# Up and down products of a conv feed-forward layer on one core: the first Strassen pair taken by hand-ordered seven products, quarter sums from one load of the rows, down rows and weights split ahead

## The chip, the cores and the metric

The kernel runs on one core of one Trainium2 chip. The metric is the device time of one execution in microseconds (us), the median of several runs. The profile is one execution, taken by the hardware profiler.

## The reference

One layer of a streaming encoder on 1056 tokens (1024 of a prompt and 32 of a decode group, which share the weights). It mixes tokens by a gated linear attention and a banded softmax attention, then runs a convolutional feed-forward network, then a gated embedding. Everything is float32. The change lies in the feed-forward part:

```python
h = rms_norm(x, g_pre_ffn)                      # D_MODEL = 1024
a, g = split(h @ w_up, [D_FF])                  # D_FF = 2816
gx = concat([conv_s0, g], axis=1)
gc = conv_b + sum(conv_w[i] * gx[:, i:i + T] for i in range(3))
y = (gelu(gc) * a) @ w_down
x = x + rms_norm(y, g_post_ffn)
```

Outputs are the layer's rows, the newest attention keys and values, and the two new states.

## The kernel before

**Number format.** Float32 products are made of two reduced operands per value: `hi` is a rounded copy (ScalarE), `lo` is the value less `hi` (VectorE or GpSimd), and a block product is three matmuls: hi times hi, hi times lo, lo times hi. Every tile that TensorE reads has to be split so first, the weights as well as the rows.

**Layout.** Rows are kept transposed: 128 features by 1056 tokens, 8 such tiles for 1024 features (KT = 8, HK = 4 is half of them). `hh` and `hl` hold the split rows of the normed input. The 5632 columns of w_up are 22 pairs f (FT = 22): 128 columns of g (called gx) and the 128 of a (called av).

**Two kinds of up product.** A plain pair is 2 x 3 = 6 products (j picks g or a, three token chunks of 352), each 8 x 3 = 24 matmuls of 352 columns: `up_plain` (L1212) makes pairs 0 to 2 in 18 products, chunks 0 and 1 first, `up_one` (L1201) makes pair 3 (UP_PLAIN = 4). `plain_out` (L1191) copies each product out of PSUM on ScalarE. From pair 4 on, `up_strassen` (L1286) splits rows and weights in quarters and makes a pair by seven products instead of eight (Strassen's scheme in Winograd's form), each 4 x 3 x 2 = 24 matmuls of 264 columns. Its row operands are b11, b21, b22 (quarters of `hh`, `hl`) and the sums t1 = b12 - b11, t2 = b22 - t1, t3 = b22 - b12, t4 = b21 - t2. Its weight operands are quarters and four sums (L1295), each split on ScalarE (L1302) and VectorE (L1303). Results go out of PSUM pairs `two` by sums on VectorE and copies on ScalarE (L1374, L1386).

**Where the sums come from.** The normed rows are also spilled to DRAM (`d_hn`, by the norm, L1095). `quarter_sums` (L1250) loads two tiles for each k of 4 from there (L1242) and makes t1 and t2 (L1256, L1257); `quarter_third` loads them again for t3 (L1267); `quarter_last` loads them a third time for t4 (L1278 to L1280), and writes t4's split over the place of b12 in `hh`/`hl`. Tiles for the loads are two buffers `hn`.

**Activation.** `activate` (L1159) makes the convolution (ScalarE L1164, VectorE L1165 and L1166), the Gelu (ScalarE L1169) and the product with a (VectorE L1170, L1171), then writes the result rows to DRAM (`d_b`, GpSimd's queue). `row_sums` (L1176) later makes quarter sums of them for the down product.

**Order.** Each engine runs its instructions in the order of its queue. The order of TensorE, VectorE and ScalarE is the order of the code wherever `tc.manual_schedule` is entered; it ends behind `up_plain`, and a scheduler sets the order of `up_one` to the last but one `up_strassen`. The last pair and the down product are in code order again. `norm_part` gives the steps of the norm of the last chunk to the first nine plain products; `plain_rest` is stepped behind products 11 to 17 and makes t1, t2 and the activation of pair 0. SyncE's queue carries loads, GpSimd's the loads and stores of `d_b`.

**Down product.** It too is made by seven products. Its row operands are entries e: two row tiles of 528 columns, loaded by GpSimd's queue from `d_b` (`load_entry`, L1434 when written for an up stage tile or `uraw`) and split (`split_entry`, L1446 ScalarE, L1447 VectorE). Weights come per unit u (`load_weights`, `split_weights`, L1456 and L1457), even units into `whi`/`wlo`, odd ones into `dhi`/`dlo`. `ahead(m)` lets the last up pair split the first four entries and unit 0's weights between its products; `last_up[2]` is the rest of that pair's sums (L1367, L1368, L1332 to L1334). `down_unit(u)` makes a unit's matmuls (L1527). `places` names the four PSUM pairs in the order in which the units' chains use them.

Of the kernel before, what the change touches and what calls it, by code (L numbers as in the profile page):

```python
# [98 lines left out]
UP_PLAIN = 4  # L99
# [10 lines left out]
def emit(tc, a):  # L110
# [920 lines left out]
    def norm_steps(tmp, c, z, acc, g, resid, keep, g_next, dst, spill=None):  # L1031
# [60 lines left out]
        for i in range(KT // 2):  # L1092
            times(i, g_next, rstd(s))
            if spill is not None:
                po.dma_start(both(spill, i), zs[i])  # L1095
            ac.activation(dst(i)[0], zs[i], AF.Copy)
            if i:
                low_half(i - 1)
            yield
# [60 lines left out]
    def activate(f, gx, av):  # L1160
        gc = tl(fp, [P, GW - 2], tag="gc", bufs=1)
# [6 lines left out]
        po.tensor_copy(convo[:, f, 2:4], gx[:, GW - 2 : GW])  # L1168
        ac.activation(gc, gc, AF.Gelu_apprx_tanh)  # L1169
# [31 lines left out]
    def up_one(f):  # L1201
        gx, av = up_buffers(f)
        for j in range(2):
            hi, lo = weights(a["w_up"][f + FT * (1 - j)], ve)
            for c in range(NC):
                s = chunk(c)
                ps = ps_mm()[:, : s.stop - s.start]
                product(ps, hi, lo, [(k, k) for k in range(KT)], lambda k: hh[:, k, s], lambda k: hl[:, k, s])
                plain_out(gx, av, j, s, ps)
        return gx, av  # L1210

    def up_plain():  # L1212
# [3 lines left out]
        for i, (f, j, c) in enumerate(steps):  # L1216
# [7 lines left out]
            if i < 9:  # L1224
                norm_part(UP_STEPS[i])
            elif i >= 11:
                next(rest, None)
            if i % 2 == 0 and 1 + i // 4 < 3:
                up_weights(1 + i // 4, i // 2 % 2)
            if i == 8:  # L1230
                rest = plain_rest(bufs)
            plain_out(gx, av, j, s, ps)
# [6 lines left out]
    def quarter_rows(k):  # L1239
        b = [tl(sp, [P, T], tag="hn", bufs=2) for i in range(2)]  # L1240
        for i in range(2):
            dma.dma_start(b[i], d_hn[k + HK * i])  # L1242
        return b[0][:, one], b[0][:, two], b[1][:, one], b[1][:, two]

    def quarter_split(n, k, t):
        h, l = (v[:, k] for v in XS[n])
        ac.activation(h, t, AF.Copy)
        ve.tensor_tensor(l, t, h, op=ALU.subtract)

    def quarter_sums():  # L1250
        for n in ("t1", "t2"):
            XS[n] = [tl(sp, [P, HK, HT], F32R, tag=n + x) for x in "hl"]
        for k in range(HK):
            b11, b12, b21, b22 = quarter_rows(k)
            t1, t2 = [tl(sp, [P, HT], tag="xs", bufs=2) for i in range(2)]
            ve.tensor_tensor(t1, b12, b11, op=ALU.subtract)  # L1256
            ve.tensor_tensor(t2, b22, t1, op=ALU.subtract)  # L1257
            quarter_split("t1", k, t1)
            quarter_split("t2", k, t2)
            yield  # L1260

    def quarter_third():
        XS["t3"] = [tl(sw, [P, HK, HT], F32R, tag="t3" + x) for x in "hl"]
        for k in range(HK):
            b11, b12, b21, b22 = quarter_rows(k)
            t = tl(sp, [P, HT], tag="xs", bufs=2)
            ve.tensor_tensor(t, b22, b12, op=ALU.subtract)  # L1267
            quarter_split("t3", k, t)

    def quarter_last():  # L1270
        XS["b11"] = [t[:, up1, one] for t in (hh, hl)]
        XS["b21"] = [t[:, up2, one] for t in (hh, hl)]
        XS["b22"] = [t[:, up2, two] for t in (hh, hl)]
        XS["t4"] = [t[:, up1, two] for t in (hh, hl)]
        for k in range(HK):
            b11, b12, b21, b22 = quarter_rows(k)
            t = tl(sp, [P, HT], tag="xs", bufs=2)
            ve.tensor_tensor(t, b12, b11, op=ALU.subtract)  # L1278
            ve.tensor_tensor(t, b22, t, op=ALU.subtract)
            ve.tensor_tensor(t, b21, t, op=ALU.subtract)  # L1280
            quarter_split("t4", k, t)

    ROW_JOBS = {min(2 * i + 3 + (i < 2) * (2 - i), FT - 2): row_sums(i, hn_tile) for i in range(FH - 1)}

    def up_strassen(f, ahead=None):
        raw = [raw_weight(), raw_weight() if f == UP_PLAIN else tl(sw, [P, KT, P], tag="sraw", bufs=2)]  # L1286
# [115 lines left out]

    def plain_rest(bufs):
        nonlocal sp
        zp.release()
        sp = pool("sp", side="right")
        yield from quarter_sums()
        activate(0, *bufs[0, 0])
        yield
# [3 lines left out]
    order.__exit__(None, None, None)  # L1413
    uw.release()
    sw = pool("sw")
    for f in range(3, UP_PLAIN):
        open_[f, 0] = up_one(f)
    quarter_third()
    for f in range(1, 3):
        activate(f, *open_[f, 0])  # L1420
    quarter_last()
    for f in range(3, UP_PLAIN):
        activate(f, *open_[f, 0])
    repsum((0, 0, 4))
    for f in range(UP_PLAIN, FT - 1):
# [60 lines left out]
    for e in range(2):  # L1486
        load_entry(e, hn_tile)
    last_up = up_strassen(FT - 1, ahead)
# [35 lines left out]
    places = [chain(j) for j in (3, 2, 0, 1)]  # L1524
# [192 lines left out]
    for e in range(4, 7):  # L1717
# [4 lines left out]
    load_entry(7)  # L1722
# [5 lines left out]
    split_weights(1)  # L1728
    activate(FT - 1, *last_up[:2])
# [6 lines left out]
    for u in range(len(UNITS)):  # L1736
        if u:
            down_unit(u, MID.get(u))
        if u + 2 < len(UNITS):
            load_weights(u + 2)  # L1740
        if 0 < u < len(UNITS) - 1:
# [338 lines left out]
```

## Time and profile before

| | |
|---|---|
| median of 3 runs | 1980.6 us (1978.6 to 1981.62) |
| profiled execution | 1979.3 us |
| its span in the profile | 1977.6 us |
| granted TensorE clock, mean | 0.991 of full speed |
| TensorE busy | 1925.8 us, 97% of the span |
| VectorE, ScalarE, GpSimd busy | 64%, 48%, 23% |
| plain up products | from about 1155 to 1253 us of the span |
| up products by seven | to 1631 us |
| down product | from 1631 us |

Times within the trace count from the start of the span. A group row gives line, engine, operation, tiles and shapes, then busy us and mean ns of one instruction, then the idle time before them and what ended it. A row of waits gives engine, tile and line, then what it waited for: us in total, times, the longest. The mean of a matmul is its latency; matmuls are pipelined, so their rate is read from their number in a full window.

### The profile page before, as it was taken

To read this page: it belongs to the slowest core of one execution; us is meant where nothing else is said; L and a number is where in the kernel's file an instruction comes from. 1 tells how busy PE (TensorE), PEld (TensorE's weight loads), DVE (VectorE), ACT (ScalarE), POOL (GpSimd) and SP (SyncE) were. 2 spreads that over 40 slices of the span, in tenths; PEclk is the share of its full clock that TensorE was granted. 3 is DMA by queue.
4 is the path that set the end of the run, shared out by engine and by line. 5 is a ranking of instruction groups with operands and counts; after the bars stand their busy time and mean duration, and the time that the engine had idled before them with its cause. 6 is when DMAs were issued, how large, how long until landed. Compare 5 with 4: busy or idle time off the path is not lost.

```text
span 1977.6 us, 34638 instructions
## 1 busy us (share of the span) xinstructions
PE 1925.8 (97%) x13584; PEld 1888.0 (95%) x13584; DVE 1260.6 (64%) x2500; ACT 943.2 (48%) x1706; POOL 462.5 (23%) x556
## 2 busy tenths in 40 slices
PE   9999999999999999999999999999999999999996
PEld 8999999999999999999999999999999999999996
DVE  6556556456366475466655677787777776456777
ACT  6356455455364463564434455333333445445444
POOL 2423333232112121211120111232122222115211
PEclk9999999999999999999999999999999999999998
DMA  7323345353444221226787247654334348556679
GB/s 265 100 86 121 100 132 143 99 147 104 113 146 115 81 66 60 97 87 236 255 291 241 89 160 232 218 180 137 130 128 138 123 162 306 183 185 200 202 233 222
DMA packets 107582, 312.04 MB, mean 158 GB/s; under 512 B 13268, under 2 KB 35612, under 8 KB 107292
## 3 DMA queue, kind: packets, MB, share of 16 engines
q1 hardware_dynamic: 81612, 222.99, 34.1%
q0 software_dynamic: 24976, 85.96, 14.6%
q8 instruction: 106, 1.74, 0.4%
q10 hardware_dynamic: 832, 0.90, 0.1%
q14 instruction: 56, 0.46, 0.1%
HBM read 226.34 MB, written 106.52 MB: 168 GB/s over the span
## 4 chain that ended last, share of the span: by engine, by line
PE 69%; DVE 11%; issue 10%; DMA 4%; ACT 4%; POOL 1%; SPq 0%; POOLq 0%; ACTq 0%; DVEq 0%
PE mm L230 10%; PE mm L229 10%; PE mm L231 10%; PE c L1527 7%; PE two L1312 6%; PE two L1313 6%; PE two L1314 6%; DMA hn<-d_hn 3%; PE aux L1527 2%; PE two L835 2%; PE one L601 2%; DVE z L1633 1%; PE one L559 1%; PE two L543 1%; PE one L849 1%
## 5 line engine op out<-in xcount | busy, mean ns | idle before, releaser
L231 PE MATMUL mm<-xh,wlo 128*128 128x352 f32 x1248 | 413.7, 331 | 0.0
L229 PE MATMUL mm<-xh,whi 128*128 128x352 f32 x1248 | 412.9, 331 | 0.0
L230 PE MATMUL mm<-xl,whi 128*128 128x352 f32 x1248 | 410.5, 329 | 0.0
L209 POOL TENSOR_TENSOR wlo<-raw,whi 128x512 fp32r<-128x512 f32 x128 | 181.0, 1418 | 686.8 <-ACT whi L208 630.5
L229 PEld LDWEIGHTS mm<-xh,whi 128*128 128x128 f32 x1248 | 236.1, 189 | 1.9 <-DVE ev L460 0.8
L230 PEld LDWEIGHTS mm<-xl,whi 128*128 128x128 f32 x1248 | 235.7, 189 | 1.7 <-issue 0.3
L231 PEld LDWEIGHTS mm<-xh,wlo 128*128 128x128 f32 x1248 | 235.5, 189 | 1.3
L1312 PE MATMUL two<-mh,whi 128*128 128x264 f32 x576 | 163.1, 287 | 5.8 <-ACT av L1193 2.4
L1314 PE MATMUL two<-mh,wlo 128*128 128x264 f32 x576 | 164.5, 287 | 0.0
L1313 PE MATMUL two<-ml,whi 128*128 128x264 f32 x576 | 164.2, 286 | 0.0
L208 ACT ACTIVATE whi<-raw 128x512 fp32r<-128x512 f32 x140 | 87.0, 628 | 149.7 <-PE mm L230 90.9
L1527 PE MATMUL c<-mh,wlo 128*128 128x264 f32 x438 | 124.5, 284 | 0.8 <-DMA wlo<-d_g 0.8
L1527 PE MATMUL c<-ml,whi 128*128 128x264 f32 x438 | 124.1, 283 | 0.9 <-DVE ml L1447 0.9
L1527 PE MATMUL c<-mh,whi 128*128 128x264 f32 x438 | 124.5, 284 | 0.0
L1312 PEld LDWEIGHTS two<-mh,whi 128*128 128x128 f32 x576 | 108.6, 190 | 6.7 <-ACT av L1193 2.7
L1314 PEld LDWEIGHTS two<-mh,wlo 128*128 128x128 f32 x576 | 109.8, 191 | 0.0
L1313 PEld LDWEIGHTS two<-ml,whi 128*128 128x128 f32 x576 | 109.7, 190 | 0.0
L460 DVE TENSOR_TENSOR ev<-mm,rstd 128x352 f32<-128x352 f32 x120 | 61.3, 519 | 50.4 <-PE mm L231 46.7
L1527 PEld LDWEIGHTS c<-mh,wlo 128*128 128x128 f32 x438 | 82.2, 188 | 1.5 <-DMA wlo<-d_g 1.5
L1527 PEld LDWEIGHTS c<-ml,whi 128*128 128x128 f32 x438 | 82.5, 188 | 1.1 <-DVE ml L1447 1.1
L1302 ACT ACTIVATE whi<-ws 128x512 fp32r<-128x512 f32 x72 | 45.3, 628 | 80.2 <-PE two L1313 48.1
L1527 PEld LDWEIGHTS c<-mh,whi 128*128 128x128 f32 x438 | 82.5, 188 | 0.0
(516 smaller groups left out, 5459.4 us busy)
## 6 DMA issues: line engine op xcount, KB each, us to landing
raw<-in_w_in SPq DMA_DIRECT2D x52, 512.0 KB, 3.7
uraw<-d_b POOLq DMA_DIRECT2D x34, 528.0 KB, 5.0
raw<-in_w_up SPq DMA_DIRECT2D x27, 512.0 KB, 3.6
hn<-d_hn SPq DMA_DIRECT2D x24, 528.0 KB, 4.9
d_b<-av POOLq DMA_DIRECT2D x44, 264.0 KB, 2.7
d_s<-in_w_down POOLq DMA_DIRECT2D x16, 704.0 KB, 7.9
draw<-d_s SPq DMA_DIRECT2D x16, 704.0 KB, 4.1
hn<-d_b POOLq DMA_DIRECT2D x40, 264.0 KB, 3.9
```

Source lines behind the costliest of these rows:

```text
L208: ac.activation(hi[-1][:, d], raw[:, b], AF.Copy)
L209: eng.tensor_tensor(lo[-1][:, d], raw[:, b], hi[-1][:, d], op=ALU.subtract)
L229: pe.matmul(ps, h, xh(kt), start=(first and i == 0), stop=False)
L230: pe.matmul(ps, h, xl(kt), start=False, stop=False)
L231: pe.matmul(ps, l, xh(kt), start=False, stop=(last and i == n - 1))
L460: return lambda ps, s: ve.tensor_tensor(t[:, s], ps, rstd(s), op=ALU.mult)
L601: pe.matmul(ps[:, j0 * P : j1 * P], vs[:, k, vd], got[x][:, k - kb, j0:j1], start=(i == 0 and x == "h"), stop=(i == len(work) - 1 and x == ...
L1302: ac.activation(h, x, AF.Copy)
L1312: pe.matmul(ps[:, j, :HC], w[0][:, k], x[0][:, k, s], start=st, stop=False, skip_group_check=True)
L1313: pe.matmul(ps[:, j, :HC], w[0][:, k], x[1][:, k, s], start=False, stop=False, skip_group_check=True)
L1314: pe.matmul(ps[:, j, :HC], w[1][:, k], x[0][:, k, s], start=False, stop=sp_, skip_group_check=True)
L1527: pe.matmul(ps, w, x, start=st, stop=sp_, skip_group_check=True)
```

## The change

- UP_PLAIN is 3: `up_one` is gone, and pair 3 is made by `up_first`, seven products in the code's own order, with weights and activations of pairs 0 and 1 written between them. `order.__exit__` moves behind it. Its products run X by b11, V by b21, Y by t2, Z by t1, V by t3, X by b22, V by t4.
- The rows are loaded once per k (`quarter_load`, L1239 of the changed file) into tiles `hx`, `gc` and two `hn`, and summed in place: t1, t2, t4. t1 and t2 are split at once. t4 goes raw to DRAM (`d_t4`), and is read back by two loads (L1265) and split once b12's place in `hh` is free. t3 is made by GpSimd (`third_sum`, L1268) from four loads of half rows (L1265).
- The activation is a generator of two steps (convolution; Gelu and product). `plain_rest` is stepped from product 8 on and behind `plain_out`. The last chunk's norm takes its tiles in the order 0, 2, 1, 3.
- Down transition: entry 2 goes into the tile `hx`, entries 3 and 4 into `hn`, each loaded one step earlier; unit 1's weights are split and unit 2's loaded ahead of the last up pair's remaining sums; unit 2's are split between the two steps of the last activation; `places` is (1, 0, 2, 3) instead of (3, 2, 0, 1).

ScalarE before, about the end of the plain products and the start of the first seven products (Gelu L1169, plain evictions L1193 to L1199 into av and gx, split of a t sum L1247, weight split L1302, convolution L1164, product eviction L1374):

```order
L1169 ACTIVATE gc_13103<-gc_13103 128x1058
L1193 ACTIVATE av_12878<-mm_12980 128x352
L1247 ACTIVATE t3h_13058<-xs_13088 128x528
L1164 ACTIVATE gc_13154<-gx_12877,vec_70 128x1058
L1193 ACTIVATE av_12878<-mm_13006 128x352
L1302 ACTIVATE whi_13244<-ws_13209 128x512
L1169 ACTIVATE gc_13154<-gc_13154 128x1058
L1302 ACTIVATE whi_13273<-raw_13169 128x512
L1193 ACTIVATE av_12878<-mm_13032 128x352
L1247 ACTIVATE mh_10372<-xs_13118 128x528
L1302 ACTIVATE whi_13304<-ws_13302 128x512
L1374 ACTIVATE p_2133_13177<-two_13179 128x528
```

And after, in the same place (L1176 is the Gelu, L1170 the convolution, L1201 to L1207 plain evictions, L1294 weight splits and L1331 the first eviction of `up_first`; t3h and mh are the splits of t3 and t4):

```order
L1176 ACTIVATE gc_12791<-gc_12791 128x1058
L1201 ACTIVATE av_12529<-mm_12867 128x352
L1294 ACTIVATE whi_12941<-ws_12939 128x512
L1170 ACTIVATE gc_12946<-gx_12372,vec_70 128x1058
L1247 ACTIVATE t3h_12901<-hn_12754 128x1056
L1331 ACTIVATE p_2089_12907<-two_12909 128x528
L1294 ACTIVATE whi_12978<-ws_12937 128x512
L1247 ACTIVATE t3h_12901<-hn_12823 128x1056
L1294 ACTIVATE whi_13014<-ws_13012 128x512
L1294 ACTIVATE whi_13048<-ws_13046 128x512
L1294 ACTIVATE whi_13104<-raw_12586 128x512
L1247 ACTIVATE mh_10372<-hn_12984 128x2x528
```

The last plain eviction no longer stands behind a Gelu that comes after the last plain products; a split of t3 stands ahead of the weights w3, w4 and w22; both halves of t4 are split in one place.

SyncE's queue before, from the third round of row loads (hn) on to the weights of the seven products (raw):

```order
L1242 DMA hn_13114<-d_hn_11241 128x1056
L1242 DMA hn_13115<-d_hn_11241 128x1056
L1242 DMA hn_13124<-d_hn_11241 128x1056
L1242 DMA hn_13125<-d_hn_11241 128x1056
L1242 DMA hn_13134<-d_hn_11241 128x1056
L1288 DMA raw_13406<-in_w_up 128x1024
L1242 DMA hn_13135<-d_hn_11241 128x1056
L1242 DMA hn_13144<-d_hn_11241 128x1056
L1288 DMA raw_13657<-in_w_up 128x1024
L1242 DMA hn_13145<-d_hn_11241 128x1056
L1288 DMA raw_13908<-in_w_up 128x1024
```

And after, from the last whole rows through half rows and t4 (d_t) to the weights of pair 4 (raw, sraw):

```order
L1239 DMA hn_12715<-d_hn_11241 128x1056
L1265 DMA hx_12752<-d_hn_11241 128x2x528
L1265 DMA hn_12754<-d_hn_11241 128x2x528
L1265 DMA hn_12823<-d_hn_11241 128x2x528
L1361 DMA sraw_13167<-in_w_up 128x1024
L1265 DMA hx_12833<-d_hn_11241 128x2x528
L1361 DMA sraw_13404<-in_w_up 128x1024
L1265 DMA hn_12984<-d_t_1997_12191 128x2x528
L1265 DMA hn_13019<-d_t_1997_12191 128x2x528
L1361 DMA raw_13166<-in_w_up 128x1024
L1361 DMA raw_13403<-in_w_up 128x1024
```

The row loads are fewer; t4's loads stand ahead of raw of pair 4.

VectorE before, at the down transition (ml is a split of an entry, L1367 to L1334 the last up pair's sums, dlo unit 1's weights):

```order
L1447 TENSOR_TENSOR ml_10373<-hn_17499,mh_10372 128x1056
L1447 TENSOR_TENSOR ml_10373<-uraw_17618,mh_10372 128x1056
L1447 TENSOR_TENSOR ml_10373<-uraw_17620,mh_10372 128x1056
L1367 TENSOR_TENSOR c_2632_17353<-p_2631_17352,two_17369 128x528
L1368 TENSOR_TENSOR gx_17348<-gx_17348,c_2632_17353 128x528
L1332 TENSOR_TENSOR gx_17348<-c_2632_17353,two_17370 128x264
L1333 TENSOR_TENSOR gx_17348<-c_2632_17353,two_17370 128x232
L1334 TENSOR_TENSOR gx_17348<-c_2632_17353,two_17370 128x32
L1457 TENSOR_TENSOR dlo_17707<-draw_17611,dhi_17706 128x512
L1457 TENSOR_TENSOR dlo_17711<-draw_17611,dhi_17710 128x512
L1457 TENSOR_TENSOR dlo_17715<-draw_17611,dhi_17714 128x384
```

And after (L1565 entries, L1575 weights, L1440 to L1405 the sums):

```order
L1565 TENSOR_TENSOR ml_10373<-hn_17465,mh_10372 128x1056
L1565 TENSOR_TENSOR ml_10373<-hn_17498,mh_10372 128x1056
L1575 TENSOR_TENSOR dlo_17628<-draw_17610,dhi_17627 128x512
L1575 TENSOR_TENSOR dlo_17632<-draw_17610,dhi_17631 128x512
L1575 TENSOR_TENSOR dlo_17636<-draw_17610,dhi_17635 128x384
L1565 TENSOR_TENSOR ml_10373<-uraw_17617,mh_10372 128x1056
L1440 TENSOR_TENSOR c_2618_17352<-p_2617_17351,two_17368 128x528
L1441 TENSOR_TENSOR gx_17347<-gx_17347,c_2618_17352 128x528
L1405 TENSOR_TENSOR gx_17347<-c_2618_17352,two_17369 128x264
L1406 TENSOR_TENSOR gx_17347<-c_2618_17352,two_17369 128x232
L1407 TENSOR_TENSOR gx_17347<-c_2618_17352,two_17369 128x32
```

Unit 1's weights moved ahead of entry 5 and of the last pair's sums, and entries 3 and 4 come from `hn`.

```diff
-UP_PLAIN = 4
+UP_PLAIN = 3
...
-        for i in range(KT // 2):
+        left = []
+        for i in range(KT // 2) if c < NC - 1 else (0, 2, 1, 3):
...
+        yield
         ac.activation(gc, gc, AF.Gelu_apprx_tanh)
...
-            elif i >= 11:
-                next(rest, None)
...
             if i == 8:
                 rest = plain_rest(bufs)
-            plain_out(gx, av, j, s, ps)
+            if i >= 8:
+                next(rest)
...
+    def quarter_load(k):
+        b = (hn_tile(), hn_tile()) if k % 2 else (odd_tile(), tl(fp, [P, GW - 2], tag="gc", bufs=1)[:, :T].rearrange("p (k t) -> p k t", k=2))
+        for i in range(2):
+            dma.dma_start(b[i], d_hn[k + HK * i].rearrange("p (k t) -> p k t", k=2))
+        XS["rows", k] = b
+    def quarter_first(k):
+        x, y = XS["rows", k]
+        ve.tensor_tensor(x[:, 0], x[:, 1], x[:, 0], op=ALU.subtract)
+        one_ = quarter_split("t1", k, x[:, 0])
+        ve.tensor_tensor(y[:, 1], y[:, 1], x[:, 0], op=ALU.subtract)
+        two_ = quarter_split("t2", k, y[:, 1])
+        ve.tensor_tensor(y[:, 0], y[:, 0], y[:, 1], op=ALU.subtract)
+        po.dma_start(d_t4[k], y[:, 0])
+        one_()
+        two_()
+    def halves(src, k, n, h=slice(0, HT)):
+        t = XS[n] = odd_tile() if n[0] == "b12" else hn_tile()
+        dma.dma_start(t, src[k : k + 2, :, h].rearrange("k p t -> p k t"))
+    def third_sum(j):
+        po.tensor_tensor(XS["b22", j], XS["b22", j], XS["b12", j], op=ALU.subtract)
...
+        for k in range(HK):
+            quarter_first(k)
+            if k < 2:
+                quarter_load(k + 2)
+            elif k == 2:
+                halves(d_hn, 0, ("b12", 0), two)
+                halves(d_hn, HK, ("b22", 0), two)
+            if k == HK - 1:
+                act = activation_steps(0, *bufs[0, 0])
+                next(act)
+            yield
+        halves(d_hn, HK + 2, ("b22", 1), two)
+        next(first)
+        third_sum(0)
+        halves(d_hn, 2, ("b12", 1), two)
+        yield
+        next(act)
...
+    next(first)
+    next(act)
+    lo = third_split(0)
+    next(first)
+    third_sum(1)
+    lo()
+    halves(d_t4, 0, ("t4", 0))
+    lo = third_split(1)
+    next(first)
+    lo()
+    halves(d_t4, 2, ("t4", 1))
+    next(first)
+    next(first)
+    next(first)
+    fourth(0)
+    fourth(1)
+    next(first)
+    next(act)
+    order.__exit__(None, None, None)
...
         if m < 5:
             split_entry(m - 3)
-            load_entry(m - 1, hn_tile)
+            load_entry(m, hn_tile)
...
+    load_entry(2, odd_tile)
...
-    places = [chain(j) for j in (3, 2, 0, 1)]
+    places = [chain(j) for j in (1, 0, 2, 3)]
...
-    for e in range(4, 7):
+    for e in range(5, 8):
         load_entry(e)
...
     split_entry(4)
-    load_entry(7)
+    split_weights(1)
+    load_weights(2)
     split_entry(5)
     load_entry(8)
     last_up[2]()
     slots.append((more[:, :, 0], more[:, :, 1]))
     down_unit(0)
-    split_weights(1)
-    activate(FT - 1, *last_up[:2])
+    act = activation_steps(FT - 1, *last_up[:2])
+    next(act)
+    split_weights(2)
+    for i in act:
+        pass
```

More of the change, by code (lines that the diff above doesn't have):

```diff
@@ L1262, in quarter_third @@
[L1262 to L1281, printed above, removed]
@@ L1400, in emit @@
     sp = None
+    first = up_first()
     def plain_rest(bufs):
@@ L1412, in emit @@
     open_ = up_plain()
-    order.__exit__(None, None, None)
+    repsum((0, 0, 4))
     uw.release()
     sw = pool("sw")
[L1416 to L1419, printed above, removed]
-        activate(f, *open_[f, 0])
[L1421 to L1425, printed above, removed]
+    XS["t3"] = [tl(sw, [P, HK, HT], F32R, tag="t3" + x) for x in "hl"]
+    act = activation_steps(1, *open_[1, 0])
+    next(first)
[14 more added lines that the diff above has]
+    fourth(1)
+    next(first)
+    next(act)
+    order.__exit__(None, None, None)
+    for f in range(2, UP_PLAIN):
+        activate(f, *open_[f, 0])
+    activate(UP_PLAIN, *XS["first"])
+    for f in range(UP_PLAIN + 1, FT - 1):
         up_strassen(f)
```

138 lines of the change are left out of this document (105 added, 33 removed).

## The prediction

> **What bounds the kernel now.** I read the page first, then the stretch of the up product by windows, then what TensorE waited for there, then the clock.
>
> ```profile
> span 1977.6 us, 34638 instructions
> PE 1925.8 (97%) x13584; PEld 1888.0 (95%) x13584; DVE 1260.6 (64%) x2500; ACT 943.2 (48%) x1706; POOL 462.5 (23%) x556
> PE 69%; DVE 11%; issue 10%; DMA 4%; ACT 4%; POOL 1%; SPq 0%; POOLq 0%; ACTq 0%; DVEq 0%
> ```
>
> TensorE is busy 97% of the span and makes 69% of the chain that ended last. An edit helps by fewer matmuls, by a gap closed, or by a clock kept up. The windows of the stretch that the change rewrites (columns: length, busy time and number of instructions of each engine, granted clock, DMA share, GB/s):
>
> ```profile
> 1190.00:1230.00 40.00, 40.00 (x249) 40.00 (x248) 28.44 (x43) 19.90 (x36) 6.42 (x14) 1.00 0.70 231
> 1256.00:1268.00 12.00, 12.00 (x88) 12.00 (x88) 8.15 (x14) 2.94 (x5) 1.08 (x2) 0.86 0.63 213
> 1280.00:1301.00 21.00, 18.75 (x139) 18.54 (x140) 18.27 (x31) 7.21 (x12) 12.23 (x19) 0.92 0.61 202
> 1301.00:1321.50 20.50, 20.50 (x171) 20.50 (x169) 15.21 (x25) 7.66 (x12) 4.78 (x12) 1.00 0.51 172
> 1321.50:1342.00 20.50, 20.50 (x171) 20.50 (x170) 15.78 (x25) 7.51 (x12) 5.15 (x12) 1.00 0.53 164
> ```
>
> The first row is plain product, full: 40.00 / 249 = 0.161 us a matmul of 352 columns. The last two are seven products, full: 41.00 / 342 = 0.120 us a matmul of 264. Between them TensorE loses time; what it waited for from 1225 to 1300:
>
> ```profile
> PE two L1312 <- ACT av L1193: 2.4, 1, 2.4
> PE two L1312 <- ACT p L1374: 2.0, 1, 2.0
> PE two L1312 <- ACT mh L1247: 1.2, 1, 1.2
> PE two L1312 <- DVE gx L1334: 0.2, 1, 0.2
> ```
>
> That is 5.8 us idle in four gaps. The second cost is the clock; slices of 3.41 us around the two large gaps and the third:
>
> ```profile
> 1253.62:1257.03 3.41, 1.56 (x12) 1.56 (x13) 2.30 (x5) 2.33 (x4) 2.29 (x2) 1.00 0.66 213
> 1257.03:1260.44 3.41, 3.41 (x18) 3.41 (x17) 3.41 (x6) 0.72 (x2) 0.72 (x2) 0.50 0.73 240
> 1260.44:1263.85 3.41, 3.41 (x30) 3.41 (x30) 1.52 (x3) 1.04 (x2) 0.35 (x1) 1.00 0.83 307
> 1277.51:1280.92 3.41, 2.24 (x18) 2.03 (x17) 2.84 (x5) 0.73 (x2) 0.89 (x2) 1.00 0.17 68
> 1287.75:1291.16 3.41, 1.39 (x12) 1.18 (x11) 3.30 (x6) 2.58 (x4) 1.61 (x3) 1.00 0.94 275
> 1291.16:1294.58 3.42, 3.42 (x17) 3.42 (x17) 3.42 (x6) 1.12 (x2) 1.49 (x4) 0.50 0.58 210
> ```
>
> Where TensorE was busy 1.56 and 1.39 of 3.41 us, the next slice ran at 0.50 and started 18 and 17 matmuls instead of 30; where it was busy 2.24, the clock stayed. The two halved slices cost (12 + 13) x 0.120 = 3.0 us. So 5.8 + 3.0 = 8.8 us are lost here beside the work itself.
>
> **Why the gaps stand there.** ScalarE around the first gap (start, length, line, tiles, idle time before), then around the second:
>
> ```profile
> 1253.46 1.09 ACT L1169 ACTIVATE gc<-gc 128x1058 f32<-128x1058 f32 x1 [1.83 <-DVE gc L1166]
> 1254.45 0.61 ACT L1302 ACTIVATE whi<-raw 128x512 fp32r<-128x512 f32 x1
> 1254.97 0.44 ACT L1193 ACTIVATE av<-mm 128x352 f32<-128x352 f32 x1
> 1255.32 0.64 ACT L1247 ACTIVATE mh<-xs 128x528 fp32r<-128x528 f32 x1
> ...
> 1288.58 1.27 ACT L1164 ACTIVATE gc<-gx,vec 128x1058 f32<-128x1058 f32 x1 [3.89 <-DVE gx L1394]
> 1289.76 0.59 ACT L1374 ACTIVATE p<-two 128x528 f32<-128x528 f32 x1
> ```
>
> The last plain eviction (L1193) stands behind a Gelu (L1169) that idled 1.83 us for VectorE; the seven-product block after it needs that PSUM. In the second gap the eviction L1374 stands behind a convolution start (L1164) that idled 3.89 us. The third gap (1.2) is the split of t4 (L1247), which waits for rows loaded for the third time:
>
> ```profile
> L1242 SPq DMA_DIRECT2D hn<-d_hn x24: 319/320/673, 1197.8 to 1272.9; - x24
> DMA to landing us min/median/max: 3.9/4.9/7.0
> ```
>
> **The change, part by part.** All times are of the profiled execution, 1979.3 us (span 1977.6), which is 1.3 below the median of the runs, 1980.6.
>
> *Fewer matmuls.* Pair f=3 was 6 products of 24 matmuls: 144 x 0.161 = 23.2 us. Now it is 7 x 24 = 168 x 0.120 = 20.2 us. **-3.0.** This is certain as far as TensorE stays fed.
>
> *The four gaps and two halved slices.* The first gap goes: the new block's first product waits only for the eviction of the 17th of 18 plain products, and no plain block follows. The t4 rows are no longer computed behind three loads each. The second gap came of work of VectorE that had gathered (18.27 busy of 21.00, quoted above); the activations of pairs 0 and 1 now stand inside the plain products and the new block. **-8.8** if nothing takes their place.
>
> *VectorE.* Removed: 4 x 10 sums and splits of 528 columns. Added: 4 x 5 of them, 4 splits of 1056, 7 more weight sums and splits, and 6 PSUM sums for f=3. Rows for these:
>
> ```profile
> L1256 DVE TENSOR_TENSOR xs<-hn 128x528 f32<-128x528 f32 x4 | 2.8, 705 | 2.6 <-DMA hn<-d_hn 2.6
> L1303 DVE TENSOR_TENSOR wlo<-ws,whi 128x512 fp32r<-128x512 f32 x24 | 16.5, 686 | 0.0
> 1636.89 2.62 DVE L1447 TENSOR_TENSOR ml<-uraw,mh 128x1056 fp32r<-128x1056 f32 x2 [3.45 <-ACT mh L1446]
> ```
>
> That is 40 x 0.70 = 28 out, and 20 x 0.70 + 4 x 1.31 + 13 x 0.70 = 28 in: no relief in sum, only another place. So I cost it at nothing by itself; its cover is the 11 us of each 40 that VectorE is idle in the first window above.
>
> *Loads.* 24 loads of 528 KB become 8, 4 of half rows and 2 of t4, with 4 writes of t4 (264 KB). Traffic falls, in windows with a DMA share of 0.6 to 0.7: nothing, or a small gain that I don't count. The order of the last norm chunk (0,2,1,3) and the step at i >= 8 change no count; their cover is the same idle quarter of VectorE.
>
> *New waits in the fixed order.* E is the end of the plain products. The chain to t3: the step with the first third_sum stands behind the 16th of 18 products; GpSimd starts it when its two half-row loads have landed, which I put at E-4 (their tiles come free about E-9, and 4.9 to land). Then third_sum 2.5, the load of b12 of the other half into the tile that it frees 4.9, third_sum 2.5, then on ScalarE the t3 split 1.1 and, behind it in the queue, the split of the weight w3 0.6, then VectorE's part 0.7. Prices:
>
> ```profile
> L652 POOL TENSOR_TENSOR ev<-ev,ev x4: 2462/2480/2696, 183.2 to 424.4; 128x1056 f32<-128x1056 f32 x4
> L209 POOL TENSOR_TENSOR wlo<-raw,whi x128: 1263/1290/3110, 27.1 to 1039.5; 128x512 fp32r<-128x512 f32 x128
> 1635.77 1.09 ACT L1446 ACTIVATE mh<-uraw 128x1056 fp32r<-128x1056 f32 x1 [4.21 <-DMA uraw<-d_b]
> ```
>
> E - 4 + 2.5 + 4.9 + 2.5 + 1.1 + 0.6 + 0.7 = E+8.3. The t3 product is the fifth of f=3 and starts at E + 4 x 2.9 = E+11.7 (24 x 0.120 = 2.9), so 3.4 us are to spare. The upper end: L209 reaches 3.11 where 1.29 is its median, a factor of 2.4, so a third_sum could take 6.0, and a load 7.0: E-4 + 6.0 + 7.0 + 6.0 + 2.4 = E+17.4, which is 5.7 late. The next chain is t4: its two loads go into the tiles that the t3 splits free, and the raw weights of f=4 stand behind them in SP's queue. I estimate the second t3 split's low half, behind w3's on VectorE, to end at about E+11; 4.5 for a load gives t4's second landing at E+15.5, f=4's weights about E+17, split (0.6 + 0.7) by E+18 to E+19; t4 starts at E+17.5, with f=4's first products set among its matmuls. So I expect 1 to 2 us of stalls there. Ends: 0.5 (all but the last split in time) and 5.7 + 1.5 (t3 late and one halved slice). **+2.0**, nearer the low end because the medians leave 3.4 to spare; each gap is then short of the idle 3.41 - 1.56 = 1.85 us that halved the clock above.
>
> [...]
>
> *Down transition.* Entries 2 to 4 are loaded earlier, into tiles of the up stage, and unit 1's weight split moves from behind the rest of the last up pair to ahead of it. What TensorE waited for from 1625 to 1650, with VectorE in between:
>
> ```profile
> PE c L1527 <- DVE dlo L1457: 1.6, 1, 1.6
> PE c L1527 <- DVE ml L1447: 0.9, 1, 0.9
> ...
> 1641.59 1.76 DVE L1457 TENSOR_TENSOR dlo<-draw,dhi 128x512 fp32r<-128x512 f32 x3
> ```
>
> The 0.9 came of entry 4, whose load (L1434) landed just before 1635.77, when ScalarE had idled 4.21 for it. It is now loaded two entries ahead. The 1.6 came of the weight split that ended its wait behind entry 5 and the sums of the last up pair; it now stands ahead of both. What is late next is entry 5, still loaded as entry 4 was and used one entry later, and the sums of the last up pair, queued behind entry 5, whose PSUM the reordered places use last. Gain 0 to 2.5; I take **-2.0**.
>
> Sum: -3.0 - 8.8 + 2.0 - 2.0 = -11.8. 1979.3 - 11.8 = 1967.5, and with 1.3 to the median **1968.8 us**. 0.2% of the time, 4 us, is about what a measurement of this kernel can tell from no change.
>
> **The rivals.**
>
> *The stalls move (0.15).* t3 comes 3 to 6 us late because third_sum is slowed and both loads take 5 to 7. That is 5.7 idle and one or two halved slices at 1.5, 2 more at t4: about 9.5 in place of 2.0. For it: L209's tail, and that ScalarE has w3 queued behind the t3 split. Against: both ends must come together. Time 1968.8 + 7.5 = 1976.3.
>
> *The halved slices stay (0.05).* The clock could follow something other than the gaps, which happen to stand just ahead of both slices. Then 3.0 of the 8.8 remain: 1971.8. For it: nothing but that two cases are few. [...]
>
> *Slower (0.08).* The fixed order now holds seven products of f=3 in one line with ScalarE and VectorE: one late third_sum stops w3, w4 and w22, the t4 loads, and behind them in SP's queue f=4's weights. At the upper ends t3 is 5.7 late, two halved slices follow (3.0), t4's loads land 7.0 after the delayed splits, some 4 late, with another halved slice (1.5), and f=4's weights 2 later still. That is 16.2 new against the 13.8 taken away: 1980.6 + 2.4 = 1983.0. It decides from about 14 us of new idle time. Against: it needs every end at once.
>
> *The sums hold but the plain products stall (0.07).* More of VectorE's and ScalarE's work now stands between the evictions of products 9 to 18; two evictions late by 1.5 each, with one halved slice (1.5), give 4.5: 1973.3. Against: the first window above is full, and VectorE is idle for 29% of it.
>
> **How the numbers follow.** The forecast has 0.65: its own range is -13.8 (0.5 of stalls, 2.5 at the down transition) to -6.8 (5.0 and nothing): 1966.8 to 1973.8. The range to hold 8 in 10 takes in the moved stalls, and at the low end 2 to 3 us for small gaps between those listed: 1964 to 1977. Faster by over 0.2% (below 1976.6): 0.65 + 0.05 + 0.07 + half of 0.15 = 0.84; slower 0.08; the other half of 0.15 within 0.2%: 0.08.
>
> **What would show it right or wrong.** Right: in the profile after, no wait of TensorE over 1.8 us between the plain products and the second seven-product pair, full clock in all slices there, f=3 some 20 us long, and no waits for weights or entries after the first down unit. Wrong: waits of TensorE for the t3 split or for w3's weights, which end with a GpSimd sum; a halved slice in f=3 or f=4; gaps inside the plain products. The prediction fails if the new waits add up to more than 10 us.

## The result and the profile after

The changed kernel takes 1968.57 us (median of 6 runs, 1967.13 to 1970.78), the kernel before 1980.03 us (6 runs beside it): a ratio of 0.9945, 95% interval 0.9932 to 0.9957, or 11.5 us less. The forecast was 1968.8. The profiled execution takes 1967.13 us.

The page of the changed kernel: TensorE is busy for 6.9 us less in a span that is 12.2 us shorter, and holds a larger share of the chain that ended last; "issue", 10% before, is 2%.

```profile
span 1965.4 us, 34662 instructions
PE 1918.9 (98%) x13608; PEld 1880.1 (96%) x13608; DVE 1264.1 (64%) x2499; ACT 942.0 (48%) x1699; POOL 471.1 (24%) x562
PE 78%; DVE 11%; ACT 5%; DMA 3%; issue 2%; SPq 0%; ACTq 0%; DVEq 0%
```

The stretch of pair 3 and after, by windows of the changed kernel (length, busy time and number of each engine, granted clock, DMA share, GB/s). The first two rows are pair 3 and the head of pair 4, the rest is pairs 4 to 6:

```profile
1228.46:1240.16 11.70, 11.58 (x92) 11.16 (x92) 11.06 (x12) 5.28 (x7) 5.99 (x10) 1.00 0.42 152
1240.16:1252.00 11.84, 10.02 (x71) 8.74 (x70) 10.88 (x18) 6.61 (x9) 2.95 (x4) 1.00 0.70 198
1252.00:1268.00 16.00, 16.00 (x134) 16.00 (x133) 15.81 (x25) 8.03 (x11) 4.52 (x10) 1.00 0.52 173
1280.00:1301.00 21.00, 21.00 (x175) 21.00 (x174) 17.81 (x29) 7.48 (x12) 6.43 (x14) 1.00 0.62 210
```

The clock is full in all these windows, and 1280 to 1301, which before held 139 matmuls, holds 175. What is left is the second row: TensorE busy 10.02 of 11.84. Its waits from 1225 to 1300, and the only one at the down transition:

```profile
PE two L1385 <- ACT whi L1375: 0.9, 1, 0.9
PE two L1308 <- DVE t3l L1248: 0.3, 1, 0.3
PE two L1308 <- DVE ml L1248: 0.3, 1, 0.3
PE two L1309 <- DVE wlo L1295: 0.2, 1, 0.2
...
PE c L1646 <- DVE ml L1565: 0.3, 1, 0.3
```

Where did the 12.2 us of span go? Landmarks answer that. Before, the first matmul of pair 3, of pair 5's t3 (L1312), of the first down unit and of the fourth down unit (the tile aux; the first three units, 198 matmuls, write tiles c):

```profile
1229.57 0.32 PE L229 MATMUL mm<-mh,whi 128*128 128x352 f32 x1
...
L1312 PE MATMUL two<-t3h,whi x8: 279/283/286, 1295.0 to 1297.5; 128*128 128x264 f32 x8
...
1631.20 0.29 PE L1527 MATMUL c<-mh,whi 128*128 128x264 f32 x1
...
1658.19 0.28 PE L1527 MATMUL aux<-mh,dhi 128*128 128x264 f32 x1
```

And after:

```profile
1228.46 0.28 PE L1307 MATMUL two<-mh,whi 128*128 128x264 f32 x1
...
L1385 PE MATMUL two<-t3h,whi x8: 282/285/287, 1285.2 to 1287.7; 128*128 128x264 f32 x8
...
1621.41 0.29 PE L1646 MATMUL c<-mh,whi 128*128 128x264 f32 x1
...
1646.03 0.28 PE L1646 MATMUL aux<-mh,dhi 128*128 128x264 f32 x1
```

| from | before | after | change |
|---|---|---|---|
| start to pair 3 | 1229.6 | 1228.5 | -1.1 |
| pair 3 to pair 5's t3 | 65.4 | 56.7 | -8.7 |
| to the first down unit | 336.2 | 336.2 | 0.0 |
| first three down units | 27.0 | 24.6 | -2.4 |
| rest | 319.4 | 319.4 | 0.0 |

In the profiles the change itself made 11.1 us. The 1.1 ahead of it are 1.9 less up to about 1059 us, where the kernels are alike (the profile of before had two more slices of half clock in its first 90 us), and 0.8 more from there to pair 3.

### The profile page after: what moved, and what is told of

It is laid out like the page before. It is cut to its first block, busy times and chain, and to the rows that moved or that the text cites. A ratio compares the mean times of both kernels' runs of the same rounds, so it can differ in the third digit from the quotient of the medians.

```text
span 1965.4 us, 34662 instructions
## 1 busy us (share of the span) xinstructions
PE 1918.9 (98%) x13608; PEld 1880.1 (96%) x13608; DVE 1264.1 (64%) x2499; ACT 942.0 (48%) x1699; POOL 471.1 (24%) x562
## 4 chain that ended last, share of the span: by engine, by line
PE 78%; DVE 11%; ACT 5%; DMA 3%; issue 2%; SPq 0%; ACTq 0%; DVEq 0%
PE mm L231 12%; PE mm L229 12%; PE mm L230 12%; PE c L1646 10%; PE two L1385 6%; PE two L1387 6%; PE two L1386 6%; PE aux L1646 2%; PE two L835 2%; PE one L601 2%; PE one L559 1%; PE two L543 1%; PE one L849 1%; DVE z L1061 1%; PE two L544 1%
## 5 line engine op out<-in xcount | busy, mean ns | idle before, releaser
L563 DVE TENSOR_TENSOR pt<-one,pt 128x128 fp32r<-128x128 f32 (+3 forms) x96 | 46.4, 498 | 56.5 <-ACT pt L562 56.4
```

The costliest lines, as they stand in the source:

```text
L563: ve.tensor_tensor(out[1], tv, out[0], op=ALU.subtract)
```

## The experiments

The ratio of each run is to runs of the kernel before on the same chip, to be compared with 0.9945 [0.9932, 0.9957]. Where a text says "above the changed kernel", it goes by these ratios, since the times before differ from chip to chip (medians of 1978.66 to 1980.82). "The stretch" is the time from pair 3's first matmul, or from the end of the plain products where pair 3 starts late, to pair 5's t3: 65.4 us before, 56.7 after. Three more profiles with the same instructions in the stretch, the runs that change the down transition alone, have 57.0, 57.1 and 58.1, so differences of about 1.4 us mean nothing there.

**The count alone.** The kernel before, with three plain pairs.

```diff
-UP_PLAIN = 4
+UP_PLAIN = 3
```

> The kernel before with three plain pairs and nothing else changed: pair 3 goes through the scheduler's seven products, the quarter sums still come from three rounds of row loads. My theory: 24 matmuls more of the short kind in place of 144 long ones save 3.0 us of TensorE, but the 23 us of plain products that covered the second and third rounds of loads are gone; in the kernel before t4's last split stood at 1281 us and the fourth pair's t4 is wanted at 1247, so TensorE idles 15 to 30 us, part of it with a halved clock: 1985 to 2000, slower than before. Rival (the gain comes from the count of matmuls): 1977, 3 us less than before.

Measured 1998.63 us, ratio 1.0098 [1.0082, 1.0113]. The longest of its waits from pair 3 to the down transition:

```profile
PE two L1312 <- ACT mh L1247: 7.4, 2, 4.1
PE two L1312 <- ACT whi L1302: 5.4, 1, 5.4
PE c L1527 <- ACT mh L1446: 3.1, 1, 3.1
PE two L1312 <- ACT p L1374: 2.7, 1, 2.7
```

The theory held. mh of L1247 is t4's split. The seven-product pair is no gain here while the quarter sums need three rounds of loads: the plain pair was their cover. The count's 3 us came only with the single load of the rows, which the next kernel has too.

**The order by hand.** The changed kernel with the scheduler ordering pair 3.

```diff
     open_ = up_plain()
+    order.__exit__(None, None, None)
     repsum((0, 0, 4))
...
     next(act)
-    order.__exit__(None, None, None)
```

> The changed kernel with the order written by hand ending behind the plain products, as before, so that the scheduler sets the order of pair 3 and of what stands around it. My theory: what counts is that the rows come once and early; the scheduler puts the splits in some other order, and the stalls are 3 to 8 us instead of 4.2: 1967.5 to 1972.5. Rival (the fixed order removed the stalls): 8 us or more above the changed kernel, with waits over 1.8 us and a halved clock in pair 3 or 4.

Measured 1973.23 us, ratio 0.9971 [0.9959, 0.9983]; the stretch takes 62.6 us. In its profile, with a mean granted clock of 0.991 where the changed kernel's has 0.995, two waits of over 2 us are back, and a halved slice after each:

```profile
PE two L1309 <- DVE wlo L1295: 3.8, 2, 2.8
PE two L1385 <- ACT p L1447: 2.3, 1, 2.3
```

In the stretch the fixed order is worth 5.9 us, and 5 us by the ratios, between the two theories: the rows loaded once give a part alone, and the rest comes from the order.

**The sums for t3 on VectorE.**

```diff
-        po.tensor_tensor(XS["b22", j], XS["b22", j], XS["b12", j], op=ALU.subtract)
+        ve.tensor_tensor(XS["b22", j], XS["b22", j], XS["b12", j], op=ALU.subtract)
```

> The changed kernel with the two sums for t3 on VectorE instead of GpSimd. In the changed kernel's trace VectorE's instructions beside the GpSimd sums are long (2.98 us for one whose like takes 1.32, 1.97 for one of 1.22). [...] Rival (the GpSimd sums are late themselves and set the stalls): 2 us or more less than the changed kernel. Second rival (the long instructions have another cause): they stay long.

Measured 1970.56 us, ratio 0.9942 [0.9926, 0.9958], as the changed kernel. I had put down that the two long instructions fall back, and a time within 1 us of the changed kernel. In the changed kernel GpSimd's sums and VectorE's instructions beside them (start, length):

```profile
1226.11 2.50 POOL L1268 TENSOR_TENSOR hn<-hn,hx 128x1056 f32<-128x1056 f32 x1 [4.06 <-DMA hn<-d_hn]
1232.37 2.48 POOL L1268 TENSOR_TENSOR hn<-hn,hx 128x1056 f32<-128x1056 f32 x1 [0.90 <-DMA hx<-d_hn]
...
1227.72 1.97 DVE L1177 TENSOR_TENSOR av<-gc,av 128x1024 f32<-128x1024 f32 x1 [1.45 <-ACT gc L1176]
1233.00 2.98 DVE L1171 SCALAR_TENSOR_TENSOR gc<-gx,vec,gc 128x1058 f32<-128x1058 f32 x1 [0.48 <-ACT gc L1170]
```

The same two VectorE instructions with the sums on VectorE:

```profile
1232.14 1.23 DVE L1177 TENSOR_TENSOR av<-gc,av 128x1024 f32<-128x1024 f32 x1
1236.66 1.32 DVE L1171 SCALAR_TENSOR_TENSOR gc<-gx,vec,gc 128x1058 f32<-128x1058 f32 x1 [0.47 <-ACT gc L1170]
```

They fall from 1.97 to 1.23 and from 2.98 to 1.32. The GpSimd sums were not slow (2.50 and 2.48, as L652 before); VectorE paid 2.4 us for them, as much as two sums of 1.25 cost on VectorE itself. In the profile the stretch is 1.2 us shorter, within what it varies by; the runs don't tell the two apart.

**The first weights of pair 3 late.**

```diff
-        wa11 = weight(a11)
-        wa12, la12 = weight(a12, True)
         yield
         gx, av = up_buffers(f)
+        wa11 = weight(a11)
+        wa12, la12 = weight(a12, True)
```

> The changed kernel with the first two weight splits of pair 3 not made ahead, but at the head of its first product, behind the last plain eviction. My theory: TensorE idles about 2 us at the start of pair 3, and if 1.85 us or more of that fall in one slice of the clock's 3.41 us, the next slice has half the clock, 1.5 us more; the queue of VectorE is shifted too: 2 to 4 us above the changed kernel, 1970.5 to 1972.5. [...]

Measured 1971.59 us (1968.63 to 1975.83), ratio 0.9962 [0.9948, 0.9976]. Its profile shows waits of 1.1 and 0.8 at the head of pair 3, and the clock:

```profile
1235.69:1239.10 3.41, 1.59 (x10) 1.08 (x9) 3.40 (x4) 1.50 (x3) 3.16 (x5) 1.00 0.77 261
1239.10:1242.51 3.41, 3.41 (x18) 3.41 (x17) 2.81 (x4) 2.66 (x3) 2.06 (x2) 0.50 0.96 376
```

No single wait here is over 1.1 us; TensorE was busy 1.59 of 3.41 us, and the next slice ran at 0.50. The time lies in the range of the theory. The stretch is 57.9 us, only 1.2 above the changed kernel's, though 1.9 of waits and 1.5 of clock were added; the later waits sum to 0.8 us where the changed kernel has 1.7. That VectorE had time to catch up would explain it, but is not shown.

**Half of the down edits, new places.** The kernel before with unit 1's weights ahead, the last activation in two steps, and the new order of PSUM places.

```diff
-    places = [chain(j) for j in (3, 2, 0, 1)]
+    places = [chain(j) for j in (1, 0, 2, 3)]
...
     split_entry(4)
     load_entry(7)
+    split_weights(1)
+    load_weights(2)
...
```

> The kernel before with one half of the down edits: unit 1's weights split and unit 2's loaded ahead of the last up pair's remaining sums, the last activation in two steps, the new order of PSUM places; the entries are loaded as before. My theory: the wait of 1.6 us for unit 1's weights at the down transition goes, the wait of 0.9 for entry 4 stays, so 1.6 us less than before, about 1978.5. Rival (the wait only moves to what is now queued behind the weights): 0 to 1 us less, with a new wait for entry 5 or for the sums of the last up pair.

Measured 1991.34 us, ratio 1.0056 [1.0037, 1.0076]. Both theories missed.

**The up part alone.** The changed kernel with the whole down transition as before, old places too.

```diff
-    places = [chain(j) for j in (1, 0, 2, 3)]
+    places = [chain(j) for j in (3, 2, 0, 1)]
...
     split_entry(4)
-    split_weights(1)
-    load_weights(2)
+    load_entry(7)
...
```

> The changed kernel with the down transition as it was before (entries, weights, places). My theory: the up part alone gives its 8.5 us of the profile, and the two waits of 1.6 and 0.9 stand again at the down transition: 2.4 us above the changed kernel, about 1971. Rival (the down edits gave nothing, the shift came from elsewhere): as the changed kernel, 1968.6.

Measured 1984.14 us, ratio 1.0015 [1.0002, 1.0029]: missed by 13 us.

**The old places alone.** The changed kernel with only this edit undone.

```diff
-    places = [chain(j) for j in (1, 0, 2, 3)]
+    places = [chain(j) for j in (3, 2, 0, 1)]
```

> The changed kernel with the PSUM places of the down units' chains in the old order. My theory: in the new order the first chains stand in PSUM that the last up pair has emptied, in the old the first two stand where its last sums still wait behind entry 5; TensorE idles 0.5 to 2 us more at the down transition: 1969 to 1970.5. Rival (the order of places is without effect): 1968.6 and no wait there over 0.3 us.

Measured 1980.53 us, ratio 0.9995 [0.9985, 1.0005]: 10 us above the changed kernel, five times the most that I had put down. The longest wait of these three kernels, in the order in which they stand here, is at the head of the first down unit, for the sums of the last up pair (L1338 to L1340, or L1405 to L1440):

```profile
PE c L1533 <- DVE gx L1340: 13.2, 1, 13.2
...
PE c L1645 <- DVE c L1440: 10.9, 1, 10.9
...
PE c L1646 <- DVE c L1440: 7.4, 1, 7.4
```

In the last of them the clock adds to it; from the slice in which the wait begins:

```profile
1620.21:1623.62 3.41, 1.26 (x11) 1.05 (x9) 3.41 (x6) 2.66 (x4) 0.72 (x1) 1.00 1.01 417
1623.62:1627.03 3.41, 0.00 (x0) 0.00 (x0) 2.89 (x5) 1.60 (x3) 1.13 (x2) 0.50 0.46 120
1627.03:1630.45 3.42, 1.55 (x7) 1.58 (x8) 3.18 (x6) 0.04 (x1) 1.21 (x4) 0.50 0.95 385
1630.45:1633.86 3.41, 3.41 (x17) 3.41 (x17) 2.11 (x2) 1.75 (x2) 0.14 (x2) 0.50 0.77 294
```

**Weights ahead, old places, in the kernel before.**

```diff
-    places = [chain(j) for j in (1, 0, 2, 3)]
+    places = [chain(j) for j in (3, 2, 0, 1)]
```

This is the diff to the kernel of half the down edits.

> The kernel before with unit 1's weights split and unit 2's loaded ahead of the last up pair's remaining sums and the last activation in two steps, but the PSUM places in the old order. After the runs with changed places the theory is: the order of places has to fit the PSUM pairs that the last up pair leaves last, the old order fits the kernel before, the new one the changed kernel, and it is no gain by itself. Then the wait of 13 us is gone here, the wait of 1.6 for unit 1's weights too, the wait of 0.9 for entry 4 stays: 1.6 us less than before, about 1978.8. Rival (the early weight split itself held up the last up pair's sums): a wait of several us for these sums stays, slower than before.

Measured 1978.79 us, ratio 1.0007 [0.9995, 1.0019]. The long wait is gone: in the kernel before the old order is the right one. The weights alone gain nothing, though: at the transition

```profile
PE c L1533 <- DVE ml L1453: 1.1, 2, 0.9
PE c L1533 <- ACT mh L1452: 0.7, 1, 0.7
```

the wait for the weights is gone and the entries' is longer, 1.8 us in sum where it was 2.5. These waits fall close together: TensorE was busy for 1.84 of the 3.41 us of the slice from 1637.08, the next slice ran at half clock, and the first three down units take 28.0 us, against 27.0 before.

**Old entries and weights, new places, in the changed kernel.** The up part alone, with the new places.

```diff
-    places = [chain(j) for j in (3, 2, 0, 1)]
+    places = [chain(j) for j in (1, 0, 2, 3)]
```

> The changed kernel with entries and weights of the down transition as before, but the new order of PSUM places. Theory: no long wait for the last up pair's sums; the two waits for entry 4 and unit 1's weights stand again with 1.6 and 0.9 us, so 2.4 us above the changed kernel, about 1971. Rival (entries and weights carry the whole of the transition): again a wait of 7 to 11 us and 1980 or more.

Measured 1974.52 us, ratio 0.9984 [0.9973, 0.9996], some 8 us above the changed kernel. Its waits at the transition, and the clock around them:

```profile
PE c L1645 <- DVE dlo L1575: 1.7, 1, 1.7
PE c L1645 <- DVE ml L1565: 0.9, 1, 0.9
...
1631.35:1634.76 3.41, 1.91 (x12) 1.29 (x10) 2.92 (x5) 1.81 (x4) 1.44 (x2) 1.00 0.50 130
1634.76:1638.17 3.41, 2.35 (x10) 2.35 (x11) 3.37 (x8) 1.27 (x1) 1.28 (x2) 0.50 0.78 220
1638.17:1641.59 3.42, 3.42 (x18) 3.42 (x17) 2.27 (x2) 2.13 (x3) 0.00 (x0) 0.50 0.58 196
```

The two waits are those of before. But here only 1.1 us of work lie between them, where it was 2.6: one slice takes the first and a part of the second, is busy for 1.91 of 3.41, and the next two run at 0.50. The first three down units take 30.2 us, against 24.6, so 5.6 and not 2.4. Another 2.3 of the 7.9 us between the two profiles lie ahead of pair 3, where the kernels are alike.

**Three attempts at the stalls that are left.** First, the weight sum s4 of pair 3 earlier:

```diff
         w3 = weight(plus(a11, a21, ALU.subtract))
+        s4 = plus(a12, s2, ALU.subtract)
         yield
...
-        w4 = weight(plus(a12, s2, ALU.subtract))
+        w4 = weight(s4)
```

> The changed kernel with the weight sum s4 of pair 3 made right behind s3, so that the raw weights' tile comes free about 2.4 us earlier and pair 4's weights can be loaded earlier. My theory: the wait of 0.9 us for pair 4's first weights goes to 0 to 0.3, the load then being held only by the second load of t4 ahead of it in SyncE's queue; the time falls by 0.5 to 0.9, under what the measurement tells. Rival (t4's split is as late): the wait moves to it, no change.

Measured 1971.14 us, ratio 0.9951 [0.9935, 0.9968]: no gain. The wait for pair 4's weights did not shrink but grew, and another came:

```profile
PE two L1386 <- ACT whi L1376: 1.5, 1, 1.5
PE two L1386 <- DVE av L1454: 1.3, 1, 1.3
```

Then pair 1's convolution later, alone and with the sums for t3 on VectorE:

```diff
     next(first)
-    next(act)
     lo = third_split(0)
...
     next(first)
+    next(act)
     next(first)
```

> The changed kernel with the convolution of pair 1, in pair 3's block, moved from behind the first product to ahead of the fifth. In the changed kernel's trace its two VectorE instructions (2.98 and 1.32 us) stand ahead of the splits for the third and fourth products and of t3. Theory: the stalls of pair 3 and 4 come from VectorE's queue, and about 1.5 of the 4.2 us go; under what the measurement tells, seen in the profile. Rival (the queue is full anyway, 21.94 of 23.54 us busy): the stalls move behind it, to t4 and pair 4's weights, and the sum stays at 4 us or grows.

> As the kernel with the convolution of pair 1 later, and the two sums for t3 on VectorE instead of GpSimd. With the sums on VectorE alone the stretch from the end of the plain products to pair 5's t3 was 1.2 us shorter in the profile. Theory: both add up, 2 to 3 us less than the changed kernel, 1966 to 1967. Rival (a full VectorE only moves its stalls): within 1 us of the changed kernel.

Measured 1973.01 us, ratio 0.9972 [0.9959, 0.9984], and 1973.41 us, 0.9974 [0.9964, 0.9984]: both slower than the changed kernel by 5 us, though the changed kernel itself did not run on this chip. In the profiles the stretch takes 60.7 and 58.4 us, with two halved slices and one: in the first TensorE was busy for 1.14 of the 3.41 us from 1252.83 and the next two slices ran at 0.50, in the second the mean clock is 0.97 from 1228.79 to 1252.33. The waits of the first:

```profile
PE two L1307 <- DVE gx L1348: 1.3, 1, 1.3
PE two L1308 <- DVE ml L1248: 1.3, 1, 1.3
PE two L1385 <- ACT whi L1375: 1.1, 2, 0.8
```

Four short stalls became five, three of them over 0.7 us, and two slices ran at 0.50. For the first kernel the rival held: the stalls moved and grew. For the second, theory and rival both missed; its profile, of the fastest of its 12 runs, shows 1.7 us of the 5 in the stretch, and where the rest lies is open.

## Why the prediction was right

The time and the direction were right, and each of the four terms stands, but not at its size. In the profiles they come to -2.8 - 9.9 + 4.0 - 2.4 = -11.1, where I had -11.8. That the time came out within 0.3 us is in part luck: new stalls of twice the size were made up for by larger gains elsewhere, and by slices of half clock ahead of pair 3, four before and two after, that have nothing to do with the change. The order of the last norm chunk, the earlier steps of `plain_rest` and the earlier split of unit 2's weights were not tried by themselves.

- *Fewer matmuls, -3.0.* In the trace pair 3 took 23.3 us before (1229.57 to 1252.90); a seven-product pair takes 20.5 from one t3 to the next. That is -2.8: the rates that I had read, 0.161 and 0.120, come from windows that count a matmul at both of their edges. The run with the count alone shows that the term is not one by itself.
- *Gaps and halved slices, -8.8.* From pair 4's start to pair 5's t3 before stand 42.1 us, and 264 matmuls at 20.5 / 168 are 32.2: 9.9 us were lost there. No gap had been left out. By the starts of the matmuls, where a full stretch has one every 0.122 us, the four waits of 2.4, 2.0, 1.2 and 0.2 cost 2.7, 2.3, 1.4 and 0.45: the busy time of a matmul is its latency of 0.28 us and covers the beginning of a gap. With the 3.0 of the clock that makes 9.9.
- *New stalls, +2.0.* Measured 4.0: 56.7 less 52.7 for 432 matmuls. The step that was off is the chain to t3: "then VectorE's part 0.7". GpSimd was nearly on time (the second sum ended at 1234.85, E+6.4, where I had E+5.9), and the t3 split on ScalarE directly behind it. But w3's sum itself is VectorE's, and stands behind the convolution (L1171, shown above, and L1172), w1's and t3's splits:

```profile
1236.01 1.32 DVE L1172 SCALAR_TENSOR_TENSOR gc<-gx,vec,gc 128x1058 f32<-128x1058 f32 x1
...
1240.35 0.63 ACT L1294 ACTIVATE whi<-ws 128x512 fp32r<-128x512 f32 x1 [4.37 <-DVE ws L1288]
```

  ScalarE idled 4.37 us for that sum, and w3 was whole at 1241.7, E+13.2 instead of E+8.3. VectorE is busy 21.94 of the first 23.54 us of pair 3 (the sum of the two windows above). I had costed VectorE at nothing in sum, and its busy time rose by only 3.5 us over the whole span, 2.4 of them beside the GpSimd sums; but I had not gone through its queue where the additions stand together. By the starts of the matmuls, 1.4 of the 4.0 are at the t3 product, 1.7 at pair 4's first weights and t4, for which I had 1 to 2, and 1.0 at the low halves of three other weights of pair 3, for which I had nothing.
- *Down transition, -2.0.* Measured -2.4 in the profile. The reason was half told: the earlier weight split alone gave nothing (the earlier loads alone were not tried), and the order of places had a price that I had not put down. It is no gain by itself: in the kernel before the new order made TensorE wait 13.2 us, in the changed kernel the old one costs 10. My explanation, that one Strassen pair more leaves other PSUM pairs to be emptied last, does not hold as it stands: the kernel with the count alone also has one pair more and keeps the old order, and its first down unit does not wait for those sums, its second 0.6 us. `up_first` takes four PSUM pairs where `up_strassen` takes three; whether this is what shifts them is open. And the run with the two waits put back loses 5.6 there and not 2.4, with two slices at 0.50 in it.
- *The rivals.* "The stalls move" is what happened in small, at 4.0 instead of 9.5, and the kernel with the convolution later comes near it, with 8.0. "The halved slices stay" is refuted by the trace after, where the gaps are gone and the clock is 1.00 from pair 3 to 1700 us, and by the late weights, where new waits of 1.1 and 0.8 us stand ahead of a slice at 0.50. The chain of the slower rival, a late sum on GpSimd, was not the one at risk; VectorE's queue was. Something slower than before lay in the places, which no rival of mine had. The plain products did not stall: TensorE's waits there are 2.8 us in sum, and 2.9 before.
- *The signs.* No wait was over 1.8 us (the longest 0.9) and the clock was full (1.00), as I had written. But pair 3 took 25.0 us, with four matmuls of pair 4 in it, and not some 20; and there were waits for the t3 split and for w3, of 0.5 us in sum, which ended with VectorE and not with a GpSimd sum.

## What to carry to other kernels

Closing a gap paid twice here: behind slices of 3.41 us that were busy for 1.56 and 1.39 us the next one ran at 0.50 and cost another 1.5 us each, and behind the one busy for 2.24 us it did not. Two waits of 1.6 and 0.9 us cost 2.4 us before, in two slices busy for 2.53 and 1.86 us with 1.00 behind both; waits of 1.7 and 0.9 us, the first and a part of the second in one slice, cost 5.6 in the kernel with old entries. So look at TensorE's work by slices, in matmuls that start there, and not at the longest gap. When work moves from one engine's idle time to another place, go through the queue of the engine that feeds the next step, instruction by instruction, and not through sums over the stretch. And a table of buffers that was matched to a rotation has to be matched again when what rotates through them changes: check who empties each last.

## What the runs showed of the hardware

*The clock.* In the profiles before and after, every stretch at one granted clock, but for the last, takes 3.41 us or a whole multiple of it, from 3.41 to 1515.52 us (444 times 3.41). Over the profiles of the 14 kernels, I set the busy time of TensorE in each slice recorded at full clock beside the clock of the next slice. Of the slices busy for less than 45%, all 58 were followed by half clock; of 45 to 50%, 7 of 10; of 50 to 60%, 3 of 18; of 60 to 75%, 4 of 120; above, none. The profiles before and after have 6 of 6, 2 of 2, 1 of 4 and 0 of 18 of these. In the up and down products from 1230 to 1940 us, where a full slice starts 28 matmuls, their number tells it better: of the slices that start 10 or fewer, all 16 were followed by half clock, of 11 or 12, 2 of 3, of 13 or more, none (before: one of 9 and one of 12 starts were, two of 13 were not; after: the fewest are 15, full clock behind it). The slice with 1.91 us busy in the kernel with old entries, which starts 10, was followed by half clock, and the slice around the wait of 1.6 us before, with 1.86 busy and 13 starts, was not.

Where the edges of the slices fall differs from profile to profile: half clock begins at 7.75, 82.84 and 434.42 us of the span before, and at 8.54 and 431.80 after. The changed kernel and six of its variants have the same instructions ahead of pair 3, and still 1 to 5 slices of half clock there: with one or two, pair 3 starts at 1227.0 to 1228.5 us, with four at 1230.7 to 1230.8, with five at 1234.0, up to 7 us apart. In the slowest run of the late weights, the one profiled (1975.83 us), 7.6 of the 8.7 us above the changed kernel's profile lie ahead of the plain products' end.

*GpSimd and VectorE.* In the changed kernel, beside the two sums on GpSimd of 2.50 and 2.48 us, the two instructions of VectorE that began while a sum ran took 0.74 and 1.66 us longer than with the sums on VectorE; the sums still had 0.89 and 1.85 us to run. I had expected GpSimd to be the one that waits. Over the eight profiles with these sums on GpSimd there are 15 such instructions, and each took longer than its like elsewhere by the time that the sum still had to run, less 0.13 to 0.21 us. Where a split on VectorE (L1295) had begun first and ran 0.67 or 0.68 us into the sum, in the kernels with old places and late weights, the sum took 3.01 us instead of about 2.5. One split (L1248, in the kernel with the scheduler's order) fits neither: it began 0.18 us before the sum and still took 3.79 us instead of 1.25.
